# A delta-rule recurrence run over all eight heads at once, chunk by chunk, with its inputs prepared earlier and kept in DRAM

## The chip, the cores and the metric

The kernel runs on one core of one Trainium2 chip. The metric is the device time of one execution in microseconds.

## The reference, cut to what matters

Two layers, T = 1024 positions, D = 1024, all float32. Each layer makes three gated branches from one projection of the normed input and adds a projected mixture to the residual:

```python
h = rmsnorm(x, norm_g); proj = h @ w_in           # 1024 x 10256, split into the parts below
a = layernorm(dwconv31(a_val * sigmoid(a_glu)));  y_a = silu(a) * silu(a_z)      # 512 channels
q, k, v = silu(dwconv4(qkv));  q, k = l2norm(q) / sqrt(128), l2norm(k)           # 8 heads of 128
beta = sigmoid(b_beta);  g = -exp(a_log) * softplus(b_alpha + dt_bias)
o = gated_delta_rule(q, k, v, beta, g)            # per head: a chunked scan, each chunk a triangular
                                                  # solve, then S = d*S + k_dec^T v_new, o from S
y_b = rmsnorm(o, onorm_g) * silu(b_z)             # 1024 channels
y_c = gelu(c_u) * (tril(c_ws) @ layernorm(gelu(c_v)) + c_bs) * silu(c_z)         # 512 channels
gates = sigmoid(gate_logits)                      # 3 x 1024 channels
merged = gates[0]*(y_a @ a_proj) + gates[1]*(y_b @ b_proj) + gates[2]*(y_c @ c_proj)
x = x + merged @ w_out                            # after both layers: a final rmsnorm
```

## The kernel before, in words

Activations lie with channels on the 128 partitions and positions in the free dimension. A large product is made in float32r as three passes (high x high, high x low, low x high parts of both operands), so a step of a product is three matmuls of 128x512. A weight tile comes from DRAM into one of three `wr` buffers, ScalarE copies its high part and GpSimd subtracts the low part (`split`), into one of five `W` buffers. `U` hands out 24 units of 4 KB per partition, in rotation; `hrings` holds eight 8 KB buffers for the split input `hT` and what follows it. PSUM has four `pg` banks (large products), two `pa` and two `pr`.

A layer runs in stages:

1. Two plain column tiles (`half_first`), the sums of blocks of h, then **the pairs** (`pairs`): two column tiles of `w_in` at a time, by a seven-product block scheme (`STEPS`, 7 x 12 = 84 matmuls for what plainly takes 96), 28 steps per pair. VectorE adds the products together (L364, L367) and carries the convolutions' taps, doled out per step (`TAPS_FAST`, `todo.tap`). GpSimd makes the weights' sums and low parts. Thirty-one pairs: values, gates, z, conv inputs, k, q, v and, at the end, `N_LATE` = 3 more pairs of gates. What is finished goes to DRAM (`k_d`, `q_d`, `v_d`, `z_d`, `g_d`, `ya_d`, `yc_d`), as does a part of hT that the block sums overwrite (`store_b12`, `reload_b12`).
2. **The recurrence, head after head.** For each head: `head_decay` (decay matrix `gam`, on GpSimd and ScalarE's exponential), `head_keys` (transposes of k, copies, squares), `head_pairs` (products qk and kk of all 8 chunks of 128 positions, VectorE from PSUM; then blocks of 32 go to DRAM and come back in another order, `s1_d`), `head_sub` (30 small VectorE operations, then a second trip through `s2_d`), `head_fetch`, `head_inv` (six rounds of small TensorE products that make the inverse `zt`), `head_values` (transposes of q and v), `head_rec` (for each chunk the products `ks`, `pq`, `pz`, `ps`, `po`, each 128x128, one after another through VectorE and ScalarE) and `head_out` (norm, transposes, times z, to `yb_d`). `interleave` puts these steps between the filler: 16 plain gate tiles (`plain`, `product` with 48 matmuls each), then projection c. `PERIOD` = 32 filler steps lie between the starts of two heads, and the stage takes `PERIOD * H + RAMP + EXTRA` = 275 of them. The head that follows is prepared beside the one that runs.
3. The rest of projections c and a, then b (`proj_c`, `proj_a`, `proj_b`), each product times its gate tile from DRAM, added up in `mp`.
4. The output product (`out_steps`), the residual and the next layer's norm.

TensorE executes in the order written throughout. VectorE does so in the pairs, VectorE and ScalarE in the recurrence; the other queues are ordered by the framework's scheduler, which is told of priorities. All DMAs are issued from the SyncE queue (SP) in order, and a DMA waits there for the data it stores and for the buffer it fills.

## Time and profile before

| | |
|---|---|
| time, median of 3 runs (lowest, highest) | 2714.35 us (2713.1, 2715.22) |
| the profiled execution: time, span | 2714.88 us, 2713.2 us |
| busy: TensorE, VectorE, GpSimd, ScalarE | 95%, 61%, 53%, 46% of the span |
| DMA queue of SP | 316.92 MB, 38.3% of 16 engines' span |
| TensorE's mean granted clock | 0.985 |

The profile is of one execution. Matmuls are pipelined and their ends are modelled, so a busy TensorE is not one at its peak. Layer 0 ends its pairs at about 746 us and its recurrence at about 1120 us; layer 1 at about 2080 and 2457 us.

### The profile page before, as it was taken

How to read it: one execution, taken by the hardware profiler on the slowest of the kernel's cores; microseconds unless marked ns; L12 is line 12 of the kernel's file. 1: busy time of each engine (PE TensorE's matmuls, PEld its weight loads, DVE VectorE, ACT ScalarE, POOL GpSimd, SP SyncE). 2: the span in 40 equal slices, each digit the busy share in tenths (PEclk: the TensorE clock that was granted, in tenths of full speed). 3: DMA queues.
4: the chain of work that ended last, by engine and by line, in shares of the span. 5: the costliest groups of instructions: out<-in, count | busy, mean ns of one | idle time of the engine just before them, and what ended most of it. 6: DMA issues, size and time to landing. Idle time of an engine off the chain costs nothing.

```text
span 2713.2 us, 42607 instructions
## 1 busy us (share of the span) xinstructions
PE 2581.5 (95%) x15963; PEld 2127.4 (78%) x15963; DVE 1653.5 (61%) x2934; ACT 1256.8 (46%) x2996; POOL 1426.3 (53%) x1144
## 2 busy tenths in 40 slices
PE   7899999999899999999999989999998999999998
PEld 6687778878788787788867878787786878878887
DVE  6688988666545453445366888986564545444442
ACT  4433435565466665322134334365654666652221
POOL 7766667758533332363166767677674333224520
PEclk9999999999999999999999989999999999999999
DMA  4122233434633534553312223243435344445432
GB/s 155 47 63 86 86 93 123 133 102 124 189 104 109 140 106 150 173 177 130 126 65 55 66 75 94 86 155 109 125 122 180 106 124 123 114 152 187 155 124 78
DMA packets 361634, 319.64 MB, mean 118 GB/s; under 512 B 98930, under 2 KB 313556, under 8 KB 360404
## 3 DMA queue, kind: packets, MB, share of 16 engines
q1 hardware_dynamic: 361428, 316.92, 38.3%
q8 instruction: 126, 2.06, 0.3%
q14 instruction: 80, 0.66, 0.1%
HBM read 221.12 MB, written 95.75 MB: 117 GB/s over the span
## 4 chain that ended last, share of the span: by engine, by line
PE 77%; DVE 9%; POOL 4%; ACT 4%; DMA 3%; issue 3%; SPq 0%; DVEq 0%; POOLq 0%; ACTq 0%
PE ps L346 35%; PE ps L246 23%; PE ps L1261 6%; PE pa L753 2%; DVE pr L686 1%; DMA wr<-in_w_in_dram 1%; PE pr L986 1%; PE pr L1003 1%; PE pr L995 1%; DVE yc L1137 1%; POOL S L174 1%; PE ps L270 1%; PE pr L1012 1%; PE pa L802 1%; DVE nm L1075 1%
## 5 line engine op out<-in xcount | busy, mean ns | idle before, releaser
L174 POOL TENSOR_TENSOR S<-st,S 128x512 fp32r<-128x512 f32 x248 | 330.0, 1331 | 201.2 <-ACT S L173 200.8
L174 POOL TENSOR_TENSOR wl<-wr,wh 128x512 fp32r<-128x512 f32 (+2 forms) x164 | 201.5, 1245 | 357.9 <-ACT wh L173 216.4
L346 PE MATMUL ps<-hT,A 128*128 128x512 f32 x1488 | 366.3, 394 | 0.0
L686 DVE SCALAR_TENSOR_TENSOR pr<-o,dwT,pr 128x512 f32<-128x512 f32 (+7 forms) x480 | 357.1, 745 | 13.6 <-ACT pr L1057 3.4
L364 DVE TENSOR_TENSOR o<-o,ps 128x512 f32<-128x512 f32 x430 | 287.2, 682 | 117.5 <-PE ps L346 106.3
L246 PE MATMUL ps<-hT,wh 128*128 128x512 f32 x960 | 332.4, 427 | 0.0
L346 PEld LDWEIGHTS ps<-hT,A 128*128 128x128 f32 x1488 | 281.1, 190 | 59.1 <-issue 0.8
L173 ACT ACTIVATE S<-st 128x512 fp32r<-128x512 f32 x248 | 156.6, 631 | 362.8 <-PE ps L346 210.0
L174 POOL TENSOR_TENSOR A<-wr,A 128x512 fp32r<-128x512 f32 x186 | 248.1, 1334 | 26.7 <-ACT A L173 25.9
L686 DVE SCALAR_TENSOR_TENSOR pr<-o,cvT,pr 128x512 f32<-128x512 f32 (+3 forms) x288 | 211.8, 752 | 44.9 <-ACT pr L706 40.6
L346 PE MATMUL ps<-T,A 128*128 128x512 f32 x744 | 192.4, 408 | 16.8 <-DVE o L364 16.8
L246 PE MATMUL ps<-hT,wl 128*128 128x512 f32 x480 | 189.8, 396 | 0.4 <-POOL wl L174 0.3
L346 PE MATMUL ps<-hT,S 128*128 128x512 f32 x744 | 184.7, 394 | 0.0
L346 PEld LDWEIGHTS ps<-T,A 128*128 128x128 f32 x744 | 144.9, 197 | 50.1 <-issue 19.7
L173 ACT ACTIVATE A<-wr 128x512 fp32r<-128x512 f32 x186 | 117.0, 629 | 126.9 <-PE ps L346 118.0
L346 PE MATMUL ps<-T2h,S 128*128 128x512 f32 x496 | 168.3, 397 | 3.0 <-ACT T2h L173 3.0
L346 PE MATMUL ps<-T3h,S 128*128 128x512 f32 x496 | 166.7, 394 | 3.0 <-ACT o L360 3.0
L346 PE MATMUL ps<-T1h,S 128*128 128x512 f32 x496 | 165.8, 393 | 0.0
L346 PEld LDWEIGHTS ps<-hT,S 128*128 128x128 f32 x744 | 139.2, 190 | 29.0 <-issue 0.7
L246 PEld LDWEIGHTS ps<-hT,wh 128*128 128x128 f32 x960 | 152.5, 191 | 11.9
L173 ACT ACTIVATE wh<-wr 128x512 fp32r<-128x512 f32 (+2 forms) x164 | 85.6, 549 | 162.5 <-issue 113.2
L1261 PE MATMUL ps<-woh,mg 128*128 128x512 f32 x512 | 140.7, 391 | 0.0
(298 smaller groups left out, 5734.8 us busy)
## 6 DMA issues: line engine op xcount, KB each, us to landing
wr<-in_w_in_dram SPq DMA_DIRECT2D x160, 512.0 KB
g_d<-gth SPq DMA_DIRECT2D x32, 512.0 KB
g_d<-o SPq DMA_DIRECT2D x16, 512.0 KB
z_d<-o SPq DMA_DIRECT2D x16, 512.0 KB
v_d<-o SPq DMA_DIRECT2D x16, 512.0 KB
k_d<-o SPq DMA_DIRECT2D x16, 512.0 KB
q_d<-o SPq DMA_DIRECT2D x16, 512.0 KB
gam<-gc_d SPq DMA_DIRECT2D x16, 512.0 KB
```

Of the source, the lines that this page charges most:

```text
L173: act.activation(out=hi, in_=src, func=AF.Copy)
L174: lo_eng.tensor_tensor(out=lo, in0=src, in1=hi.bitcast(F32), op=ALU.subtract)
L246: pe.matmul(ps[h], lhsT=w[wi][:, k, :], rhs=rhs(h, ri, k), start=(k == 0 and i == 0), stop=(k == kt - 1 and i == 2))
L270: pe.matmul(ps[h][:, sl], lhsT=w[wi][:, k, :], rhs=rhs(h, ri, k)[:, sl], start=(k == 0 and i == 0), stop=(k == kt - 1 and i == 2))
L346: pe.matmul(ps, lhsT=wt[:, wi, k, :], rhs=blk(nb, ri, k), start=(k == 0 and i == 0), stop=(k == 3 and i == 2))
L364: dve.tensor_tensor(out=out, in0=other, in1=ps, op=ALU.add)
L686: dve.scalar_tensor_tensor(out=acc[:, lo:], in0=x[:, h * HALF + lo - s:(h + 1) * HALF - s], scalar=taps[s - 1], in1=acc[:, lo:], op0=ALU.m ...
L753: pe.transpose(tp[:, j * P:(j + 1) * P], src[:, half * 4 + j, :], ident)
L802: pe.matmul(tp[:, j], lhsT=kT[:, n], rhs=qT[:, n], start=True, stop=True)
L986: pe.matmul(ks, lhsT=kT[:, n], rhs=st, start=True, stop=True)
L995: pe.matmul(pz, lhsT=zt[:, n, :], rhs=rt, start=True, stop=True)
L1261: pe.matmul(ps[h], lhsT=mg[hh, ri, k // 4][:, k % 4, off:off + P], rhs=wo[k][wi][:, h * HALF:(h + 1) * HALF], start=(k == 0 and i == 0), s ...
```

## The change

The recurrence is no longer run head by head. Its inputs are made head by head during the pairs (`head_prep`, `head_values`, `head_sub`, `head_fetch`, `head_inv`, strung together in `whole_head`; a head starts every 56 steps from pair 18.5 on) and stored in DRAM by chunk: `kE_d`, `vn_d`, `qk_d`, `zt_d` beside `k_d`, `q_d`, `z_d`, all laid out chunk, partition, head, position, so that a head is written in rows of 512 bytes and a chunk of all heads read in rows of 4 KB. The keys' factor E is multiplied in by VectorE as it empties PSUM, in place of ScalarE's copy and GpSimd's product. The inversion's PSUM tiles move from `pr` to `pa`, since `pr` belongs to the convolutions there.

All 24 gate tiles are made as pairs, so there are 39 pairs, the last eight of them gates; `plain` and `use_gate_tile` go, and with them `store_b12` and `reload_b12`. After the pairs comes projection c alone, with `yc` and `mp` in hT's buffers; then `recurrence` over 8 chunks, each with `ks`, `pq`, `pz`, `ps`, `po` for four heads at a time, into one bank, and with projection a and the first half of projection b (positions 0 to 511) as filler at `REC_FILL` = 1.5 steps per slot. The half of b can begin when four chunks are stored. The output of a chunk (`output`, `store`) is split into SBUF directly, without `yb_d`. Then the second half of b, for which its weights are loaded and split again.

```diff
-PERIOD = 32
-RAMP = 17
+PREP_FIRST, PREP_EVERY = 18.5, 56
+REC_FILL = 1.5
+LAG_DECAY = 4
...
+    k_d, q_d, z_d, kE_d, vn_d, qk_d, zt_d = (dr.tile([NT, P, H, P], F32, name=f"{nm}_d")
+                                             for nm in ("k", "q", "z", "kE", "vn", "qk", "zt"))
...
+    def head_prep(s, r):
...
+        k_u, q_u = fetch_head(k_d, hd, "kT"), fetch_head(q_d, hd, "qT")
+        kT, qT = by_chunk(k_u), by_chunk(q_u)
+        sp.dma_start(out=gam, in_=gc_d[:, hd, :].partition_broadcast(P))
+        yield from wait(10)
...
+            tp = tok(kT, half).rearrange("p (n i) -> p n i", n=4)
+            for j in range(4):
+                n = half * 4 + j
+                act.activation(out=junk, in_=tp[:, j], func=AF.Square, accum_out=ssk[:, n:n + 1])
+            yield
+            dve.tensor_tensor(out=kE[:, hs], in0=tp, in1=bc(E[:, 1, hs, hd], 2, P), op=ALU.mult)
+            yield
+        save_head(kE_u, kE_d, hd)
...
-        p0 = pr.tile([P, HALF], F32, name="pr").rearrange("p (n i) -> p n i", n=8)
+        p0 = pa.tile([P, HALF], F32, name="pa").rearrange("p (n i) -> p n i", n=8)
...
+    def recurrence(l, r, yb, fed):
...
+        load(0, "vn", "zt", "kE", "qk", "k", "q")
+        yield
...
+            if n + 1 < NT:
+                load(n + 1, "k", "q", "vn", "zt", "kE")
...
+            def ks(g):
+                if n:
+                    p = bank(pr, "pr")
+                    for j in range(4):
+                        hd = g.start + j
+                        pe.matmul(p[:, j], lhsT=kT[:, hd], rhs=st[:, hd], start=True, stop=True)
+                    for j in range(4):
+                        hd = g.start + j
+                        dve.scalar_tensor_tensor(out=vn[:, hd], in0=p[:, j], scalar=E[:, 3, n, hd:hd + 1],
+                                                 in1=vn[:, hd], op0=ALU.mult, op1=ALU.add)
...
+            A, B = SLOTS
+            for i, (f, g) in enumerate(((ks, A), (ks, B), (pq, A), (pz, A), (pq, B), (pz, B), (ps, A), (po, A),
+                                        (ps, B), (po, B))):
+                f(g)
+                if i == 8:
+                    squares(A)
+                beside()
+                if i == 5:
+                    F(c.pop("vn"), c.pop("zt"))
+                    load_z(n)
+                    if n + 1 < NT:
+                        load(n + 1, "qk")
                 yield
...
+        def whole_head(s):
+            yield from head_prep(s, r)
+            values = head_values(s)
+            for _ in range(14):
+                next(values, None)
+                yield
+            for _ in head_sub(s):
+                next(values, None)
+                yield
+            run(values)
+            yield from wait(8)
+            yield from head_fetch(s)
+            yield from wait(8)
+            for _ in head_inv(s):
+                yield from wait(3)
+        prep = [(late(lambda s=s: whole_head(s)), int(PREP_FIRST * 28 + PREP_EVERY * s.hd), 1) for s in hs]
...
+        add_glu(3), add_z(4), add_z(6), add_gates(1), add_kq(0), add_kq(1)
         at["a_norm"] = len(specs)
...
+        add_v(0), add_az(0), add_az(2), add_kq(2), add_v(2), add_kq(3), add_gates(1)
+        add_kq(4), add_v(4), add_kq(5), add_gates(1), add_kq(6), add_v(6), add_kq(7)
+        add_gates(8)
...
+        feed = projections()
+        run(steps(feed, 8 * NT))
+        with tc.manual_schedule(engines={getattr(mybir.EngineType, e) for e in B_ENG}):
+            credit, fed = 0.0, 8 * NT
+            for _ in recurrence(l, r, yb, lambda: fed):
+                credit = min(credit + REC_FILL, 2.0)
+                while credit >= 1 and (fed < 16 * NT or len(r.stored) >= 4):
+                    credit -= 1
+                    fed += 1
+                    next(feed, None)
+        run(feed)
```

## Rows read from the trace of the kernel before

**Rows 1.** The page's first part: engine, busy us (share of the span) xinstructions.
```profile
PE 2581.5 (95%) x15963; PEld 2127.4 (78%) x15963; DVE 1653.5 (61%) x2934; ACT 1256.8 (46%) x2996; POOL 1426.3 (53%) x1144
```

**Rows 2.** The chain of waits in order of time: start us, us, what.
```profile
356.80 175.99 PE ps L346 x768
...
737.03 8.30 DMA inv<-s
...
1902.42 4.25 DMA wr<-in_w_in_dram
```

**Rows 3.** Windows, recurrence and pair stages' ends: stretch, length, busy (instructions), clock, DMA share, GB/s.
```profile
746.00:1120.00 374.00, 356.74 (x3747) 295.36 (x3748) 172.15 (x538) 228.44 (x785) 117.58 (x112) 0.99 0.44 124
...
2080.00:2457.00 377.00, 355.93 (x3747) 295.08 (x3748) 174.16 (x541) 229.36 (x787) 120.63 (x115) 1.00 0.44 127
...
704.00:750.00 46.00, 36.27 (x235) 29.59 (x233) 24.67 (x56) 21.26 (x60) 19.57 (x17) 0.93 0.71 217
2045.00:2095.00 50.00, 40.92 (x349) 33.16 (x348) 24.18 (x56) 26.72 (x75) 22.46 (x22) 0.97 0.64 209
```

**Rows 4.** The timeline of TensorE in the recurrence: start us, us, engine, line, operation.
```profile
863.98 0.60 PE L753 MATMUL pa<-ident,kT 128*128 128x128 f32 x4
864.34 0.71 PE L246 MATMUL ps<-hT,wh 128*128 128x512 f32 x2
...
866.92 0.39 PE L991 MATMUL pr<-st,qT 128*128 128x128 f32 x2
867.14 1.06 PE L802 MATMUL pa<-qT,kT 128*128 128x128 f32 x8
867.96 0.70 PE L246 MATMUL ps<-hT,wh 128*128 128x512 f32 x2
```

**Rows 5.** Groups of TensorE, 746 to 1120 us: busy, mean ns | idle before, releaser.
```profile
L958 PE MATMUL pr<-inv,gam 64*64 64x64 f32 x128 | 9.1, 221 | 0.0
...
L914 PE MATMUL pr<-inv 32*32 32x32 f32 x512 | 6.3, 199 | 11.7 <-DVE inv L910 11.7
...
L936 PE MATMUL pr<-inv,gam 32*32 32x32 f32 x256 | 5.6, 192 | 4.4 <-DVE sub L853 3.7 <-DVE inv L931 0.7
```

**Rows 6.** Groups of VectorE, 760 to 1120 us: six heads' pairs, seven heads' head_sub.
```profile
L855 DVE TENSOR_TENSOR sub<-sub 128x16 f32<-128x16 f32 (+14 forms) x105 | 34.8, 331 | 1.9
L856 DVE TENSOR_REDUCE sub<-sub 128x8 f32<-128x16 f32 (+14 forms) x105 | 24.1, 230 | 3.6
...
L824 DVE SCALAR_TENSOR_TENSOR gam<-pa,Wn,gam 128x128 f32<-128x128 f32 x48 | 13.4, 342 | 0.0
...
L803 DVE TENSOR_TENSOR qk<-pa,gam 128x512 f32<-128x512 f32 x12 | 8.3, 690 | 1.3 <-ACT junk L771 1.0 <-PE pa L802 0.3
```

**Rows 7.** Windows in the pair stage of layer 0, columns as in rows 3.
```profile
460.00:540.00 80.00, 80.00 (x355) 66.24 (x354) 54.80 (x81) 42.64 (x71) 57.73 (x46) 1.00 0.46 145
...
560.00:600.00 40.00, 35.95 (x177) 29.50 (x176) 25.71 (x42) 30.51 (x70) 24.38 (x22) 1.00 0.34 110
...
240.00:260.00 20.00, 14.72 (x59) 11.59 (x57) 18.40 (x26) 4.44 (x7) 8.83 (x8) 0.83 0.23 78
...
400.00:420.00 20.00, 20.00 (x90) 16.55 (x89) 19.50 (x30) 5.72 (x10) 14.76 (x12) 1.00 0.20 53
```

**Rows 8.** Groups of ScalarE, 760 to 1120 us.
```profile
L997 ACT ACTIVATE vh<-pr,W 128x128 f32<-128x128 f32 x64 | 23.5, 367 | 15.2 <-PE pr L995 13.1
...
L785 ACT ACTIVATE gam<-gam,ng 128x128 f32<-128x128 f32 x48 | 17.3, 392 | 0.1
...
L771 ACT ACTIVATE junk<-kE 128x128 f32<-128x128 f32 x48 | 14.8, 309 | 1.1
```

**Rows 9.** The timeline of ScalarE at a change from exponential to Silu.
```profile
610.94 1.28 ACT L717 ACT_TABLE_LOAD   x1
612.24 1.06 ACT L717 ACTIVATE o<-o 128x1024 f32<-128x1024 f32 x1
```

More of the change, by code (lines that the diff above doesn't have):

```diff
@@ L551, in drop_sum @@
                 free.rotate(len(us))
-    def reload_b12():
-        for i in range(2):
-            hT[1, i, 0] = hrings[1, i, 0].tile([P, 4, HALF], F32R, name="hT")
-            with tc.issue_after(last_load[0].ins):
-                sp.dma_start(out=hT[1, i, 0].rearrange("p k t -> p (k t)").bitcast(F32), in_=b12_d[i])
-        yield
     class Record:
@@ new lines, in head_prep @@
+        nk2 = sm.tile([P, 8], F32, name="nk2", bufs=1)
+        dve.tensor_scalar(out=nk2, in0=ssk, scalar1=EPS, scalar2=None, op0=ALU.add)
+        Wt = r.W[:, hd, :]
+        dve.reciprocal(out=Wt, in_=nk2)
+        dve.tensor_tensor(out=Wt, in0=Wt, in1=beta[:, :, hd], op=ALU.mult)
+        Wn = sm.tile([P, 8], F32, name="Wn", bufs=1)
+        dve.tensor_scalar(out=Wn, in0=Wt, scalar1=-1.0, scalar2=None, op0=ALU.mult)
+        s.nk = sm.tile([P, 8], F32, name="nk")
+        pool.tensor_tensor(out=s.nk, in0=nk2, in1=phalf, op=ALU.pow)
@@ L797, in head_pairs @@
+        yield from wait(LAG_DECAY)
+        qk_u = U("qk")
+        qk = by_chunk(qk_u)
         mT = gam
@@ L917, in head_inv @@
         yield
[L918 removed]
+        q0 = pa.tile([P, HALF], F32, name="pa").rearrange("p (n i) -> p n i", n=8)
         for n in range(NT):
@@ L1215, in proj_c @@
             th = fetch(g_d[2, m], "gcl")
-            if m in (0, 2):
-                pair = hrings[0, m // 2, 1].tile([P, 2, T], F32, name="mp")
-                mp.extend((pair[:, 0], pair[:, 1]))
-            elif m >= 4:
-                mp.append(th)
-            yield from product(w(), y_rhs(yc), 4, gate_mul(th, mp[m]), w.ahead)
-            if m < 4:
-                F(th)
-        for hi, lo in yc:
-            F(hi, lo)
+            yield from product(w(), y_rhs(yc), 4, gate_mul(th, lambda h: mp_tile(mp, h, m)), w.ahead)
+            F(th)
     def proj_a(ya, mp, w):
@@ L1229, in proj_a @@
             th = fetch(g_d[0, m], "gal")
-            yield from product(w(), y_rhs(ya), 4, gate_mul(th, th), w.ahead, done_with(ya) if m == NT - 1 else None)
-            pool.tensor_tensor(out=mp[m], in0=mp[m], in1=th, op=ALU.add)
+            yield from product(w(), y_rhs(ya), 4, gate_mul(th, lambda h: th[:, hsl[h]]), w.ahead)
+            for h in range(2):
+                out = mp_tile(mp, h, m)
+                pool.tensor_tensor(out=out, in0=out, in1=th[:, hsl[h]], op=ALU.add)
             F(th)
-    def done_with(ys):
-        return lambda k: F(*ys[k])
@@ L1425, in layer @@
-                    (steps(second_head, S_SECOND[0]), *at_step("head", S_NEXT[4], 0.5))])
-        tc_dve.__exit__(None, None, None)
-        def plain():
-            br, m = order[n_gates]
-            for i, pss in enumerate(half_first((w(),), h_rhs, 8)):
-                if i in (4, 6):
-                    w.ahead()
-                yield
-            use_gate_tile(br, m)(pss[0])()
-            for br, m in order[n_gates + 1:]:
-                yield from product(w(), h_rhs, 8, use_gate_tile(br, m), w.ahead)
-            yield from proj_c(yc, mp, w)
-            yield from proj_a(ya, mp, w)
@@ L1487, in used, with projections, more_wo @@
             wo.append((hi, lo))
-        run(proj_b(yb, mp, mg, w, used))
+        def projections():
+            yc, ya = [], []
+            load_split(yc_d, yc)
+            for h in range(2):
+                for q in range(2):
+                    mp[h, q] = hrings[h, 1, q].tile([P, 4, HALF], F32, name="mp")
+            yield from proj_c(yc, mp, w)
+            load_split(ya_d, ya)
+            yield from proj_a(ya, mp, w)
+            yield from proj_b(yb, mp, mg, w, 0, pool)
+            for p in range(4):
+                F(yb[0, 0, p], yb[0, 1, p])
+        feed = projections()
[9 more added lines that the diff above has]
+        run(feed)
+        def used(k):
+            if k % 2:
+                F(yb[1, 0, k // 2], yb[1, 1, k // 2])
+                if len(wo) < 8:
+                    load_wo()
+        def more_wo():
+            for _ in range(6):
+                load_wo()
+                yield
+        interleave(proj_b(yb, mp, mg, w, 1, dve, used), [(more_wo(), 4, 8)])
         g_bc = load_gain(norm_g[l + 1] if l + 1 < DEPTH else final_g)
```

536 lines of the change are left out of this document (252 added, 284 removed).

## Prediction

> **What bounds the kernel now.** The page's first part comes first: TensorE is busy 95% of the span and no other engine over 61% [rows 1]. A busy TensorE need not stream, so the chain of waits is read next: where nothing holds it, 768 matmuls of 128x512 take 175.99 us, 0.229 us each with some records missing; the 175.99 us of pieces and the windows (90 started or ended in 20 us) both fit 0.227 us, which I use; a step of three is 0.68 us [rows 2, 7]. By that price a stage is split into work and standing still.
>
> The recurrence of layer 0 takes 374.0 us (layer 1: 377.0) [rows 3]. It holds 275 filler steps by the code (PERIOD x 8 + RAMP + EXTRA), 825 matmuls or 187 us. The heads' own TensorE work: a lone f32 128x128 matmul occupies 0.22 us, four in a row 0.82, four transposes 0.36 [rows 4]. Eight heads need 38 recurrence matmuls each (304 x 0.22 = 67), 24 groups of four for qk and kk (20), 228 transposes (21) and eight inversions. The inversion's six products cost at most four times L914's 6.3/8 and twice L958's 9.1/8, 5.4 us a head, 43 in all [rows 5]. Sum 151; I take 148, since the first head's qk and some edges fall outside. So 374 - 187 - 148 = 39 us stand still, 42 in layer 1. The groups name 16 of them: inversions waiting for VectorE (11.7 and 4.4 us) [rows 5]. The other 23 us, 6% of the stage, are seams between short f32 work and filler. Just ahead, at the end of the pairs, 46.0 - 36.27 = 10 us and 50.0 - 40.92 = 9 us are idle; the chain there holds 8.30 us of one inv load [rows 2, 3]. These 39 + 10 + 42 + 9 = 100 us are all that a reordering here can win; later stages stream.
>
> **The change, part by part.** *Gate tiles as pairs.* Sixteen gate tiles per layer leave `product` (16 x 48 = 768 matmuls) and become eight pairs (8 x 84 = 672): 96 fewer, 192 for both layers, at 0.227 us: **-43.6 us**. This is the one certain term, since both forms stream at the same price. The matmuls of projection b stay 384: halves change their order and load and split its weights twice, eight more loads of 512 KB with two ScalarE and two GpSimd operations each. That hides behind 24 matmuls (5.4 us) per tile; uncovered it would be a load of 4.25 us each [rows 2], 34 per layer. The removed b12 store and reload, yb round trip and plain start lie in the stalls already taken out.
>
> *The old stalls go: -100 us.* What is late instead is costed in three places.
>
> *(a) Head preparation in the pair stage.* Its TensorE work is moved, not added: 24 transposes 2.2, qk and kk 3.3, inversion 5.4, about 10.5 us a head after rounding down. A head starts every 56 steps, so two pairs (38.1 us) and one head share 48.6 us. A head asks VectorE for L855 34.8/7, L856 24.1/7, L824 13.4/6, L803 8.3/6 and again 1.4 for the decayed keys, now made there: 5.0 + 3.4 + 2.2 + 1.4 + 1.4 = 13.4 us plus small ones [rows 6]. Two pairs with q, k, v convolutions ask 68% of 38.1, or 26 us (54.80 of 80) [rows 7]. Together 39.5 of 48.6, 81%. ScalarE: 8 exponentials 2.9, 16 squares 4.9, 8 copies 2.9, some 13 small copies priced like the squares 4.0, 14.7 at least; two pairs ask 53% of 38.1, 20.3 [rows 7, 8]. Together 72%. GpSimd gives the product of the keys away and gains nothing else of size; it stands at 72% (57.73 of 80). The head's DMAs come along: four loads and four stores of 512 KB and the small ones of the two block passes, 4 MB or 84 GB/s beside today's 145 at 46% share [rows 7], 230 at about 73%. All go through SP in order, so a store that waits for its engine holds up the weights behind it, which have three load buffers and five split pieces of lead. No engine is over its time on average. But VectorE and TensorE keep the order written, the pieces of two heads alternate on the two banks of `pa`, and the fifteen steps of `head_sub` put 8.4 us of VectorE work into 10 us that also carry taps. So the cost is waiting. Bounds: no reason allows less than the 16 us per layer that today's inversions wait for VectorE; at worst six heads' 291 us lose the 26% of the window at 240 us, where VectorE was busy 18.40 of 20: 77 us [rows 7]. Nearest is the window at 560 us, where layer norm works through transposes, ScalarE and `pa` as the heads will: 4.05 of 40 us idle, 10% [rows 7]. On the nine convolution pairs among the heads (9 x 24.3 us) that is 22; two heads in gate pairs add their inversion waits, 4. I take **26 per layer**.
>
> *(b) Two hand-overs.* yc can be loaded only into hT's buffers, the last of which frees with the last pair; ya only into yc's. A load of 512 KB costs 4.25 us where it was the wait, the reload through SP's queue 8.30 for 128 KB [rows 2]; a split behind it needs one VectorE operation of 1024 columns (twice L803's 0.69) and one ScalarE operation of about 1.1, 2.5 us [rows 6]. A four-tile product covers 18 matmuls, 4.1 us, before the last tile is needed: 4.25 + 2.5 - 4.1 is 3 us each, 6 for both, to 16 if both meet a queue like inv's. I take **8 per layer** (4 to 16).
>
> *(c) The recurrence.* A chunk has 40 f32 matmuls in fours (8.2), 8 transposes (0.7) and 15 filler steps (10.2): 19.1 us, eight of them 153. Between `ks` and `pz`, `pz` and `ps`, `ps` and the next `ks` lie three slots of 1.8 us; a link needs 0.82 plus four operations of 0.34 to 0.37 [rows 4, 6, 8], 2.3 us: covered. Seams at 6% cost 9. The eight tiles per chunk that share `pa` collide about twice for 0.5 us, 8. Filler ends when proj_a does, in chunk 4, since proj_b may not start before four chunks are stored: eight slots bare, where sixteen copies (5.9) and the chain outlast 7.3 us of matmuls by about 4. Start and tail 3. **24 per layer**; low 15 without the collisions, high 52: a chunk loads seven tiles of 512 KB and 1.4 MB for the filler, 4.9 MB; at the 217 GB/s of the stretch where loads were the wait, 22.6 us, 28 more [rows 3].
>
> Sum: 2713.2 - 43.6 - 100 + 2 x (26 + 8 + 24) = 2685.6 us span; the execution lay 1.7 over its span, and 0.5 over the median: **2687 us**.
>
> [...] Exponentials and the convolutions' Silu need different tables: in the trace a load of 1.28 us stands before each change, and 612.24 - 610.94 shows nothing behind it but the load [rows 9]. Today only the first heads' exponentials meet Silu; then those of seven heads do, in two blocks each. [...]
>
> **Rivals.**
> - *Preparation chokes the pairs (the other side).* VectorE at 92% held TensorE up for 26% of the window at 240 us; at 400 us it was busy 19.50 of 20 with even work, and TensorE never stopped [rows 7]. It decides from 40 us per layer (5.0 a head); at 77 the time is 2687 + 102 = **2789**.
> - *Loads set the recurrence's pace:* 4.9 MB per 19.1 us is 257 GB/s, against 217 at 71% share today [rows 3]; large rows speak for less. 52 in place of 24: **2743**.
> - *Table changes land on TensorE's path,* because the squares and copies queued behind them hold `pa`. Two per head and layer cost 7 x 2 x 2 x 1.28 = 36, four 72: 2723 to **2759**. For: two banks; against: ScalarE has 28% left.
> - *Waits stay at their low ends:* 16, 4 and 15: 2687 - 46 = **2641**. For: the first heads' preparation in today's gate pairs.
> - *The change does not relieve anything:* the new waits eat the 43.6 us, **2709 to 2720**.
>
> **How the numbers follow.** Forecast 0.46 (2650 to 2708); low waits 0.13; nothing gained 0.08; preparation 0.16; loads 0.09; tables 0.08. A difference under 0.2% (5.4 us) is about what this kernel's measurement cannot tell from none. Faster 0.59, same 0.08, slower 0.33. Low waits end around 2630; above 2760 lies the greater part of the preparation case, 0.10. Range 2630 to 2760; the forecast's own is 2650 to 2708.
>
> **What would show it.** 3,276 matmuls at the pairs' line per layer and none of plain gate tiles; a pair stage longer by about 152 us of pairs and 67 of preparation; a recurrence near 180 us per layer beside today's 374. Wrong would be: TensorE waiting in the pairs for VectorE's `o` or ScalarE's `junk` by over 40 us per layer; `recurrence` matmuls waiting for DMA; more than 60 table loads in the stage. If the matmul count does not fall, the certain term is gone.

## The result: slower, and the profile after

The changed kernel takes **2904.03 us** (median of 4 runs, 2901.36 to 2909.61) beside 2713.72 us of the kernel before: the ratio is **1.0705, 95% interval 1.0686 to 1.0723**. The forecast was 2687 us with a range of 2630 to 2760; it missed by 217 us and has the wrong sign.

The page's first part for the changed kernel, to be read beside [rows 1]: TensorE fell from 95% to 90% of a longer span, VectorE kept its 61%.

```profile
PE 2606.8 (90%) x15771; PEld 2140.1 (74%) x15771; DVE 1772.8 (61%) x3002; ACT 1318.5 (45%) x3100; POOL 1599.6 (55%) x1320
```

Windows of the changed kernel, columns as in [rows 3]: both pair stages, what lies between the last pair and the output product in both layers, and both recurrences.

```profile
64.40:1086.30 1021.90, 912.00 (x5830) 742.25 (x5829) 686.34 (x1170) 502.82 (x1120) 621.70 (x510) 0.95 0.43 121
1499.20:2516.50 1017.30, 909.12 (x5829) 739.35 (x5828) 683.49 (x1164) 501.18 (x1118) 615.36 (x509) 0.95 0.43 122
...
1086.00:1370.00 284.00, 261.76 (x1428) 222.18 (x1427) 138.75 (x259) 119.04 (x369) 133.54 (x110) 0.96 0.57 191
2517.00:2805.00 288.00, 261.85 (x1422) 221.81 (x1422) 136.09 (x259) 120.02 (x371) 135.06 (x111) 0.95 0.56 189
1153.00:1323.00 170.00, 160.33 (x1012) 140.92 (x1011) 84.11 (x206) 84.28 (x312) 88.13 (x75) 0.98 0.52 179
2584.00:2753.00 169.00, 159.31 (x1007) 140.03 (x1006) 84.13 (x206) 84.29 (x312) 87.71 (x75) 0.98 0.52 179
```

The recurrence takes 170 and 169 us where [rows 3] have 374 and 377. From the last pair to the output product 284 and 288 us were measured. The forecast's sum has 287 to 288 there (535.9 us in layer 0 before, less 174.3 of plain tiles, 67 of preparation and 39 of standing still, and 32 of new waits), so nothing of the miss lies behind the pairs. The pair stage was to take 681.5 - 10 + 152.5 + 67 + 26 = 917 us in layer 0. By the same cut (from the first pair to the first inversion, which before begins at 745.94 us in layer 0 and at 2085.13 in layer 1) it was to take 674 - 9 + 152.5 + 67 + 26 = 910.5 us in layer 1. It takes 1021.9 and 1017.3: **105 and 107 us too much**, nearly the whole of the 217. In it TensorE is not busy for 109.9 and 108.2 us, and its granted clock is 0.95; the trace has two levels, 1.00 (from 632 to 638 us) and 0.50 (from 625 to 630 us).

What TensorE waited for in the changed kernel, both layers together (engine, tile and line, releaser: us in total, times, longest):

```profile
PE pa L726 <- DVE kE L761: 65.6, 14, 9.5
PE pa L894 <- DVE inv L890: 43.7, 14, 4.0
PE ps L230 <- ACT y L157: 21.8, 4, 8.4
PE pa L944 <- ACT inv L940: 18.5, 12, 1.9
PE ps L330 <- DVE o L348: 16.9, 7, 5.2
```

L726 are the transposes of `tok`, L761 scales the keys and is the new VectorE operation, L894 and L944 are products of the inversion. The pairs' own line L330 hardly waits for VectorE's sums: 16.9 us, as before. The groups of VectorE, 440 to 1086 us:

```profile
L838 DVE TENSOR_TENSOR sub<-sub 128x16 f32<-128x16 f32 (+14 forms) x120 | 72.6, 605 | 3.3
L839 DVE TENSOR_REDUCE sub<-sub 128x8 f32<-128x16 f32 (+14 forms) x120 | 27.6, 230 | 4.1
...
L761 DVE TENSOR_TENSOR kE<-pa,E 128x512 f32<-128x512 f32 x16 | 10.4, 683 | 7.0 <-ACT junk L759 7.0
```

The substitution's multiply (L838) takes 605 ns where [rows 6] have 331 for the same shapes; its reduce still takes 230. One such place, first in VectorE's timeline:

```profile
615.07 1.09 DVE L838 TENSOR_TENSOR sub<-sub 128x72 f32<-128x72 f32 x1
616.19 0.23 DVE L839 TENSOR_REDUCE sub<-sub 128x8 f32<-128x72 f32 x1
616.46 0.95 DVE L838 TENSOR_TENSOR sub<-sub 128x80 f32<-128x80 f32 x1
...
618.79 0.30 DVE L838 TENSOR_TENSOR sub<-sub 128x88 f32<-128x88 f32 x1
...
619.41 0.32 DVE L838 TENSOR_TENSOR sub<-sub 128x96 f32<-128x96 f32 x1
...
623.73 0.29 DVE L839 TENSOR_REDUCE sub<-sub 128x8 f32<-128x128 f32 x1
623.94 1.28 DVE L761 TENSOR_TENSOR kE<-pa,E 128x512 f32<-128x512 f32 x2
```

GpSimd's timeline at the same time:

```profile
614.77 1.29 POOL L271 TENSOR_TENSOR st<-wr,st 128x512 f32<-128x512 f32 x1
616.03 1.29 POOL L158 TENSOR_TENSOR A<-wr,A 128x512 fp32r<-128x512 f32 x1
...
618.50 0.96 POOL L882 MEMSET zt<- 128x1024 f32 x1
```

And TensorE's:

```profile
619.29 1.53 PE L330 MATMUL ps<-hT,A 128*128 128x512 f32 x6
624.67 1.12 PE L726 MATMUL pa<-ident,qT 128*128 128x128 f32 x4 [3.85 <-DVE kE L761]
...
628.15 0.63 PE L330 MATMUL ps<-T2h,S 128*128 128x512 f32 x1
628.58 0.63 PE L330 MATMUL ps<-T2l,S 128*128 128x512 f32 x1
...
637.44 0.39 PE L330 MATMUL ps<-T1l,S 128*128 128x512 f32 x1
637.66 0.39 PE L330 MATMUL ps<-T1h,S 128*128 128x512 f32 x1
```

with the windows of the two stretches behind the wait:

```profile
624.60:631.00 6.40, 6.33 (x18) 5.19 (x19) 4.83 (x8) 3.58 (x12) 2.85 (x3) 0.54 0.50 114
632.00:638.00 6.00, 6.00 (x27) 4.67 (x25) 4.30 (x8) 4.55 (x14) 4.21 (x4) 1.00 0.62 174
```

Three things are to be seen. First, the 128x72 and 128x80 multiplies end within 0.1 us of GpSimd's operations on weights (616.16 beside 616.06, 617.41 beside 617.32), while the larger 128x88 and 128x96 take 0.30 and 0.32: GpSimd writes a memset as they begin, and that does not hold them up. Over the whole execution 135 of the 240 multiplies began while GpSimd was at a weight's sum or low part; they take 0.86 us on average. The other 105 take 0.30, the 17 that began beside the memset 0.31. Second, behind the last round stand the next head's keys at 623.94. Until they are out of PSUM, TensorE stands before the next transposes (3.85 us at 624.67), although it has pair matmuls behind them in its queue. Third, when it goes on, its matmuls begin 0.43 us apart at a granted clock of 0.54, and from 632 us 0.22 to 0.23 apart at 1.00: the lower clock comes on top of the wait.

### The profile page after: what moved, and what is told of

Same layout as the page of the kernel before. It is cut to its first block, busy times and chain, and to the rows that moved or that the text cites. A ratio compares the mean times of both kernels' runs of the same rounds, so it can differ in the third digit from the quotient of the medians.

```text
span 2899.6 us, 42862 instructions
## 1 busy us (share of the span) xinstructions
PE 2606.8 (90%) x15771; PEld 2140.1 (74%) x15771; DVE 1772.8 (61%) x3002; ACT 1318.5 (45%) x3100; POOL 1599.6 (55%) x1320
## 5 line engine op out<-in xcount | busy, mean ns | idle before, releaser
L158 POOL TENSOR_TENSOR S<-st,S 128x512 fp32r<-128x512 f32 x312 | 414.2, 1328 | 263.2 <-ACT S L157 261.7
L348 DVE TENSOR_TENSOR o<-o,ps 128x512 f32<-128x512 f32 x542 | 362.2, 681 | 320.7 <-PE ps L330 306.8
L330 PE MATMUL ps<-hT,A 128*128 128x512 f32 x1872 | 488.1, 407 | 0.0
L330 PEld LDWEIGHTS ps<-hT,A 128*128 128x128 f32 x1872 | 358.9, 196 | 76.1 <-issue 0.6
L158 POOL TENSOR_TENSOR wl<-wr,wh 128x256 fp32r<-128x256 f32 (+2 forms) x132 | 154.3, 1183 | 239.2 <-ACT wh L157 128.8
L330 PE MATMUL ps<-T,A 128*128 128x512 f32 x936 | 241.7, 404 | 17.6 <-DVE o L348 16.9
L330 PE MATMUL ps<-hT,S 128*128 128x512 f32 x936 | 241.0, 397 | 0.0
L330 PE MATMUL ps<-T2h,S 128*128 128x512 f32 x624 | 225.5, 411 | 3.1 <-ACT T2h L157 3.0
L330 PE MATMUL ps<-T3h,S 128*128 128x512 f32 x624 | 226.8, 415 | 1.5 <-POOL S L158 1.2
L330 PEld LDWEIGHTS ps<-T,A 128*128 128x128 f32 x936 | 178.0, 195 | 56.8 <-issue 19.9
L330 PE MATMUL ps<-T1h,S 128*128 128x512 f32 x624 | 207.6, 392 | 0.0
L230 PE MATMUL ps<-y,wh 128*128 128x512 f32 x512 | 174.8, 421 | 26.0 <-ACT y L157 21.8
L330 PEld LDWEIGHTS ps<-hT,S 128*128 128x128 f32 x936 | 171.5, 188 | 35.1 <-issue 1.0
L282 POOL TENSOR_TENSOR st<-wr 128x512 f32<-128x512 f32 x78 | 103.1, 1322 | 151.1 <-DMA wr<-in_w_in_dram 145.8
L1298 PE MATMUL ps<-yb,wh 128*128 128x512 f32 x512 | 168.1, 410 | 7.3 <-ACT wh L157 7.3
L838 DVE TENSOR_TENSOR sub<-sub 128x16 f32<-128x16 f32 (+14 forms) x240 | 147.4, 614 | 6.5
L330 PEld LDWEIGHTS ps<-T2h,S 128*128 128x128 f32 x624 | 123.6, 198 | 30.3 <-ACT T2h L157 3.4
```

What stands on the lines that cost most here:

```text
L158: lo_eng.tensor_tensor(out=lo, in0=src, in1=hi.bitcast(F32), op=ALU.subtract)
L230: pe.matmul(ps[h], lhsT=w[wi][:, k, :], rhs=rhs(h, ri, k), start=(k == 0 and i == 0), stop=(k == kt - 1 and i == 2))
L282: pool.tensor_tensor(out=s1, in0=a21, in1=a22, op=ALU.add)
L330: pe.matmul(ps, lhsT=wt[:, wi, k, :], rhs=blk(nb, ri, k), start=(k == 0 and i == 0), stop=(k == 3 and i == 2))
L348: dve.tensor_tensor(out=out, in0=other, in1=ps, op=ALU.add)
L838: dve.tensor_tensor(out=pd[:, :, 0:i + 1], in0=bc(mb3[:, 0:i + 1, i], 1, 8), in1=tt[:, :, 0:i + 1], op=ALU.mult)
```

## The experiments

Times are of one run each where no interval is given; with them ran the kernel before, at 2710 to 2718 us. Four runs of one kernel lie 7 to 15 us apart (changed kernel, e17, e18, e19), so differences under 15 us are not read from single runs. All start from the changed kernel.

**Keys 14 steps later.**

```diff
-        yield from wait(10)
+        yield from wait(24)
         pool.affine_select(out=gam, ...
```

> Each head's first transposes and its keys come 14 steps later, so that they fall behind the previous head's substitution on VectorE instead of beside it; everything else of the head moves with them. Theory (step (a) was mis-sized, because VectorE is late with the keys while it is in the substitution and so holds both small PSUM banks): the wait of the transposes for VectorE's keys falls from 67 us in all to under 20, and the time by 40 to 90 us, to 2815 to 2865 us. Rival (the preparation's own matmuls and its transfers are the loss, wherever they lie): no change beyond 10 us, 2894 to 2914. Rival (a head's later steps are the loss, and moving the head only moves the wait): under 20 us of gain, with the wait now at another line of the head.

2939.49 us: **35 us slower**, outside all three ranges. Its waits of GpSimd, then TensorE:

```profile
POOL gam L749 <- DMA gam<-gc_d: 110.8, 14, 9.9
...
PE pa L726 <- DVE kE L761: 91.7, 14, 10.9
...
PE pa L938 <- issue: 53.7, 6, 10.2
```

The wait for the keys grew, and a new one came before the inversion's 64x64 products. So the collision with one neighbour's substitution was not the whole of it; the theory in this form fell. What GpSimd does at L749 is taken up below.

**Most of the substitution left out.**

```diff
         for i in range(1, 16):
-            dve.tensor_tensor(out=pd[...], ...)
-            dve.tensor_reduce(out=tt[...], ...)
+            if i == 1:
+                dve.tensor_tensor(out=pd[...], ...)
+                dve.tensor_reduce(out=tt[...], ...)
```

> Leaves out 14 of the 15 rounds of the substitution on VectorE (multiply and reduce), with all its transfers and steps kept. Theory (VectorE late in the substitution holds the banks): some 200 us of VectorE's work go, the wait for the keys falls under 15 us, the time by 60 to 130 us, to 2775 to 2845. Rival (the inversion's round trips over DRAM and the table loads are the loss): under 25 us of gain, over 2880. Rival (hand-overs behind the pairs): no change, 2894 to 2914.

2843.72 us, 60 less: the low end of the theory. The wait for the keys fell as told (6.8 us in all), but 176 us of VectorE's busy time bought only 60, and the inversion's wait for VectorE grew from 43.7 to 62.1.

**Keys by ScalarE.**

```diff
-            dve.tensor_tensor(out=kE[:, hs], in0=tp, in1=bc(E[:, 1, hs, hd], 2, P), op=ALU.mult)
+            for j in range(4):
+                n = half * 4 + j
+                act.activation(out=kE[:, n], in_=tp[:, j], func=AF.Copy, scale=E[:, 1, n, hd:hd + 1])
```

> The scaled keys are taken out of PSUM by ScalarE, in eight operations of 128x128 with the scale of each chunk, instead of by VectorE's two of 128x512; VectorE keeps the substitution. The result is the same. Theory: the transposes no longer wait for VectorE, that wait of 67 us goes to under 10 and ScalarE takes no more than 25 us of it, so 2815 to 2870. Rival (ScalarE is late too, with the norms' squares, the exponentials and their table loads): the wait is there under ScalarE's name, at least 45 us of it, and the time is 2885 to 2930.

2862.94 us, 41 less, inside the theory's range; but 36.1 of the 65.6 us came back under ScalarE's name, more than it allowed.

**Only the transfers of the preparation.**

```diff
-            yield from head_prep(s, r)
-            ... values, substitution, inversion ...
+            k_u, q_u = fetch_head(k_d, hd, "kT"), fetch_head(q_d, hd, "qT")
+            ... stores of k_u, q_u and v in the places of kE, qk, zt and vn ...
```

> Leaves out all that the engines do to prepare a head between the pairs, and keeps its large transfers to and from DRAM (keys, queries and values in; four arrays out); the pairs, the recurrence and the hand-overs are whole. By the forecast's own sizes this takes away 67 us of matmuls and 26 us of stalls a layer, 186 in all: 2718. Theory (the forecast's whole miss of 217 us lies in the engines' work of the preparation): 134 us of matmuls, 52 us of forecast stalls and most of the 217: 2500 to 2560. Rival (traffic of 512-byte rows, the pairs themselves, or the hand-overs hold the miss): 2690 to 2730. Between 2560 and 2690 both have a share.

2530.58 us, **373 less**. That expectation took 67 us for the matmuls, which is only the part that moved; the eight heads' whole is the forecast's 8 x 10.5 = 84, so its rival should have read 2904 - 2 x (84 + 26) = 2684, and both ranges for the theory 34 us lower. The answer is the same: windows of its two pair stages,

```profile
63.00:899.50 836.50, 786.77 (x3463) 643.00 (x3461) 531.61 (x769) 348.34 (x592) 575.98 (x446) 0.98 0.45 138
1316.00:2144.80 828.80, 785.26 (x3463) 643.05 (x3461) 525.25 (x762) 345.39 (x590) 568.53 (x445) 0.98 0.46 139
```

against 1021.9 and 1017.3 us with the heads. What the run leaves out, the engines' work of the preparation with its loads of the gates and its small block transfers, costs 185 and 189 us a layer where 84 + 26 = 110 were forecast. Of it 60 and 65 us are time in which TensorE is not busy (109.9 and 108.2 less 49.7 and 43.5). Another 31 and 34 are the clock: the trace has the lower level, 0.50, for 102 and 99 us with the heads and for 41 and 31 without, and half of the difference is lost. The rest, 94 and 90, is its matmuls at full speed beside the 84. The large transfers, rows of 512 bytes, are at most a small part of the loss: what is left of the miss without the heads is 30 and 28 us (worked out below). That part has waits of its own, which the changed kernel hardly has (1.2 us at L330):

```profile
PE ps L330 <- POOL A L158: 20.7, 10, 3.8
PE ps L330 <- POOL S L158: 14.4, 6, 3.5
```

All of them lie between 582 and 784 us and between 1831 and 2029 us, while the heads' transfers run (the last stores are issued at 779 and 2024 us), and GpSimd there waits for weights from DRAM (243.5 us in all, 145.8 in the changed kernel).

**No table loads.**

```diff
-                act.activation(out=gam[:, n], in_=gam[:, n], func=AF.Exp, scale=-1.0, bias=r.ng[...])
+                act.activation(out=gam[:, n], in_=gam[:, n], func=AF.Tanh, scale=0.0)
```

> Leaves out the decay matrix: in place of the exponential ScalarE takes the hyperbolic tangent of zero times the same tile, as many operations of the same size, so that no table has to be loaded for them. The rest is whole. Theory (VectorE's lateness and its waits are the loss): about 24 of 43 table loads go and the time stays within 12 us of 2904, 2892 to 2912, since ScalarE's waits at TensorE are 20 to 25 us in all and most of them are the length of its operations. Rival (the table loads lie on TensorE's path): 24 times 1.28 us or more, 2840 to 2875.

2885.29 us, 19 less, between the two. 30 of 43 loads go, 38 us of ScalarE's time. But the 128 operations also became shorter, 0.30 us in place of 0.39, which is another 12: so the tables are worth 19 us at most, a small part of the loss.

**No inversion.**

```diff
-        ... six products and their evacuations ...
+        for _ in range(6):
+            yield
```

> Leaves out the six products of the inversion and their evacuations (the inverse is stored as zeros), and keeps the substitution and every transfer. Theory (the inversion's waits are a loss of their own: 77 us in the pair stages of both layers beside 86 us of matmuls, and the clock that falls behind each wait): 150 to 190 us less, 2715 to 2755. Rival (the inversion only shows where VectorE is late, and what does not wait there waits at the next line): 85 to 115 us less, 2790 to 2820.

2800.27 us, 104 less, the rival's range, and no more than TensorE's busy time lost (2606.8 to 2499.2 us; 86 by the forecast's price). The first line of its waits shows why:

```profile
PE pa L726 <- DVE kE L761: 117.2, 14, 11.0
```

The heads stall nearly as long as before (65.6 + 43.7 + 18.5 us), only at one place instead of three.

**One operand in the multiply.**

```diff
-            dve.tensor_tensor(out=pd[...], in0=bc(mb3[...], 1, 8), in1=tt[...], op=ALU.mult)
+            dve.tensor_scalar(out=pd[...], in0=tt[...], scalar1=0.0, scalar2=None, op0=ALU.mult)
```

> Leaves out the substitution's product: its multiply becomes a multiply of one operand by a constant, of the same shape and as often, with the sums behind it unchanged. Theory (a multiply with two operands in SBUF waits until GpSimd's operation ends, with one it does not): its mean falls from 614 ns to under 330, some 70 us of VectorE's busy time go, and the time falls by 25 to 60 us, 2844 to 2879. Rival (the multiply is slow by its shape or its strides): its mean stays above 500 ns and the time within 10 us of 2904.

2911.51 us, no gain, and a mean of 598 ns in the stretch from 440 us, as before the edit (605): two operands are not what matters. But neither is the shape: of its 240, the 151 that began beside any GpSimd operation take 0.86 us and the 89 others 0.20. The rival's reason fell too, though its numbers came. The pair on three banks below settles it.

**VectorE's load spread.** The keys as in e3, and:

```diff
+SUB_EVERY, TAPS_LATE, LATE_FROM = 2, 0.43, 520
-                    credit += TAPS_SLOW if step // 28 in slow else TAPS_FAST
+                    credit += TAPS_LATE if step > LATE_FROM else TAPS_SLOW if step // 28 in slow else TAPS_FAST
             for _ in head_sub(s):
-                next(values, None)
-                yield
+                for _ in range(SUB_EVERY):
+                    next(values, None)
+                    yield
```

> The keys scaled by ScalarE as in the run of that name (2863 us), and VectorE's load spread: a round of the substitution every second step instead of every step, and from step 520 on the convolutions' taps at 0.43 per step instead of 0.65. The result is the same. Theory (VectorE is asked for more than a step holds for some fifteen steps of each head, and its order is fixed, so that the next head's inversion and products come late): the inversion's wait for VectorE falls from 45 us to under 20 and the time to 2800 to 2845. Rival (these waits are round trips over DRAM and between engines, as long whatever VectorE's load): 2850 to 2880.

2876.96 us, the rival's range, and no gain over the run that it starts from (2863). The inversion's wait for VectorE did fall under 20 us, but again TensorE stood 53.7 us before the 64x64 products, as in e1.

**The gates earlier.** The load of `gam` becomes the first of a head's transfers and the mask moves behind the keys; in e9 on top of e8, in e10 on top of e3:

```diff
+        sp.dma_start(out=gam, in_=gc_d[:, hd, :].partition_broadcast(P))
         k_u, q_u = fetch_head(k_d, hd, "kT"), fetch_head(q_d, hd, "qT")
-        sp.dma_start(out=gam, in_=gc_d[:, hd, :].partition_broadcast(P))
         yield from wait(10)
-        pool.affine_select(out=gam, ...)
         ...
         save_head(kE_u, kE_d, hd)
+        pool.affine_select(out=gam, ...)
```

> The run with VectorE's load spread (2877 us), and in it the load of each head's gates is the first of the head's transfers and GpSimd's mask on it comes six steps later. In that run, and in the one with later keys, TensorE stood 54 us before the inversion's 64x64 products for nothing that the trace names; in the latter GpSimd waited 111 us in all for that load, in front of the inversion's two small copies. Theory (GpSimd's queue, held by the mask, holds the inversion): the 54 us go, and with them what hangs behind: 2790 to 2840. Rival (the stall has another cause, as the small copies' own time behind the weight sums): it stays above 30 us, 2860 or more.

> The keys scaled by ScalarE (2863 us) and the earlier load and later mask of the gates, without the spread. Theory (GpSimd's wait for the gates also makes weight sums late and VectorE with them): 2835 to 2860. Rival (in this order nothing of the path stands behind the mask): 2858 to 2868.

2866.46 us (e8 had 2877) and 2855.17 (e3 had 2863), both differences too small to be read. e9 met its rival: the stall before the 64x64 products (L940) is still 44.8 us, and another stands before the products ahead of them:

```profile
PE pa L928 <- ACT inv L922: 35.2, 8, 9.0
PE pa L940 <- issue: 30.5, 4, 7.8
...
PE pa L940 <- POOL st L272: 14.3, 2, 7.4
```

e10 lies in its theory's range, which shows nothing at this size. e9's ScalarE timeline shows what the theory had left out:

```profile
592.65 1.28 ACT L775 ACT_TABLE_LOAD   x1
598.61 2.15 ACT L775 ACTIVATE gam<-gam,ng 128x128 f32<-128x128 f32 x7 [4.68 <-POOL gam L764]
600.67 1.10 ACT L872 ACTIVATE vn<-pa,nk 128x128 f32<-128x128 f32 x4
...
603.23 0.78 ACT L922 ACTIVATE inv<-pa 32x256 f32<-32x256 f32 x2
```

and TensorE's the price:

```profile
593.14 0.69 PE L918 MATMUL pa<-inv,gam 32*32 32x32 f32 x32
...
603.65 0.66 PE L928 MATMUL pa<-inv 32*32 32x32 f32 x3 [7.56 <-ACT inv L922]
```

The exponentials of the next head wait in ScalarE's queue for GpSimd's mask, and behind them stands the evacuation for which the inversion waits (an evacuation is the copy out of PSUM): a product ready at 593.83 is fetched at 603.23. The mask begins at 597.48, 10.4 us after its load was issued. For this mask the trace names no releaser; for 9 of the 16 it names the load, 73.3 us in all.

**The solution in PSUM, and its control.** Both on top of e10, e11 with the first line alone: the control with three banks for the pairs' products instead of four, and the fourth bank for the substitution's solution `tt`:

```diff
-    pg = ctx.enter_context(tc.tile_pool(name="pg", bufs=4, space=PSUM))
+    pg = ctx.enter_context(tc.tile_pool(name="pg", bufs=3, space=PSUM))
+    pt = ctx.enter_context(tc.tile_pool(name="pt", bufs=1, space=PSUM))
-        pool.tensor_copy(out=tt, in_=eye8)
+        s.tp = pt.tile([P, HALF], F32, name="pt")[...]
+        act.activation(out=s.tp, in_=eye8, func=AF.Copy)
...
-            dve.tensor_tensor(out=pd[...], in0=bc(mb3[...], 1, 8), in1=tt[...], op=ALU.mult)
-            dve.tensor_reduce(out=tt[...], ...)
+            dve.tensor_tensor(out=pd[...], in0=bc(mb3[...], 1, 8), in1=s.tp[...], op=ALU.mult)
+            dve.tensor_reduce(out=s.tp[...], ...)
...
+        act.activation(out=tt, in_=s.tp, func=AF.Copy)
```

> As the run before it, with three PSUM banks instead of four for the pairs' products; it is the control for the next one. Theory: a product takes 2.7 us and its sums 0.7 to 1.4 us on VectorE, so that three banks do while VectorE is on time: within 10 us of the run before. Rival (the fourth bank is what lets TensorE run on while VectorE is late): 30 us or more slower, with the wait at the pairs' line for VectorE's sums.

> As the control with three banks, with the substitution's solution kept in the free bank of PSUM, so that its multiply reads one operand from SBUF and one from PSUM; ScalarE copies it in and out. The result is the same. Theory (the multiply waits for GpSimd's operations because it takes both of its operands through SBUF): its mean falls from over 600 ns to under 400, VectorE gets 50 us or more back, and the time is 20 to 60 us under the control. Rival (it is slow by its shape, or the sums of weights slow it in another way): a mean above 550 ns and no gain.

2888.74 us, 34 over e10 (the rival: 38.5 us of waits for VectorE's sums where e10 has 15.6), and 2864.89, **24 under its control**. Groups of VectorE in the control,

```profile
L839 DVE TENSOR_TENSOR sub<-sub 128x16 f32<-128x16 f32 (+14 forms) x240 | 146.8, 612 | 6.5
```

and with the solution in PSUM:

```profile
L841 DVE TENSOR_TENSOR sub<-sub,pt 128x16 f32<-128x16 f32 (+14 forms) x240 | 66.6, 277 | 5.4
L842 DVE TENSOR_REDUCE pt<-sub 128x8 f32<-128x16 f32 (+14 forms) x240 | 56.8, 236 | 8.2
```

The same multiply with one operand in PSUM takes 277 ns, although 158 of the 240 began beside GpSimd's work on weights; 80 us of VectorE's time come back and bring 24.

**No taps beside the heads.** The three taps of the convolutions of q, k and v are left out:

```diff
+            if len(taps) > 3:
                 dve.scalar_tensor_tensor(out=acc[:, lo:], in0=x[...], scalar=taps[s - 1], ...)
```

> The changed kernel without the three taps of the convolutions of keys, queries and values, which are 144 VectorE operations of 0.75 us a layer; their first and last steps on ScalarE stay. Theory (the preparation stalls because VectorE is asked for convolutions and substitution at once): the waits of the heads for VectorE, 124 us in both layers, mostly go, and the time falls by 80 to 150 us, 2754 to 2824. Rival (the head's own chain between TensorE, ScalarE, VectorE and two PSUM banks is too long for the steps it has, whatever else VectorE does): under 40 us, 2864 or more.

2866.19 us, 38 less for about 216 us of VectorE's work: the rival's range. The wait for the keys is still 57.9 us; that of the inversion for ScalarE doubled to 37.9.

**Heads beside pairs without taps.** On e10, and with the solution in a bank of the convolutions in e15:

```diff
-PREP_FIRST, PREP_EVERY = 18.5, 56
+PREP_FIRST, PREP_EVERY = 21.5, 52
-        add_v(0), ..., add_kq(3), add_gates(1)
-        add_kq(4), add_v(4), add_kq(5), add_gates(1), add_kq(6), add_v(6), add_kq(7)
-        add_gates(8)
+        add_v(0), ..., add_kq(3)
+        add_kq(4), add_v(4), add_kq(5), add_kq(6), add_v(6), add_kq(7)
+        add_gates(10)
```

> The keys scaled by ScalarE and the earlier gates (2855 us), with two pairs of gate tiles moved from between the convolutions' pairs to the end, and the heads begun at pair 21.5 instead of 18.5 and every 52 steps instead of 56: the convolutions are over by pair 25, when three of eight heads have begun. The result is the same. Theory (convolutions and substitution together are too much for VectorE): 2795 to 2830. Rival (the chain of a head is too long whatever lies beside it, and heads now follow closer): 2845 to 2880.

> The run with late heads, and the substitution's solution in one of the two PSUM banks of the convolutions, which stand idle then; ScalarE copies it in and out. The result is the same. By the pair of runs on three banks this is worth 24 us. Theory: the multiply's mean falls under 330 ns and the time by 15 to 35 us against the run with late heads. Rival (beside gate pairs VectorE has time to spare, so a faster multiply is worth nothing): within 8 us.

2913.84 us, **59 more** than e10, beyond its rival's range too, and 2886.55, 27 less than e14, with the multiply at 276 ns: its theory. Relieving VectorE by this order of the pairs does not pay: in e14 GpSimd waits 127.5 us for the gates, and TensorE 43.2 us before L927 for an evacuation of ScalarE. The order, the later start and the 52 steps were changed at once, and no run separates them.

**The gates 12 steps ahead.** In e17 on top of e9; in e18 with e3's keys and the solution in PSUM, the heads where the change has them; in e19 on top of e15:

```diff
-PREP_FIRST, PREP_EVERY = 18.5, 56
+PREP_FIRST, PREP_EVERY = 506.0 / 28, 56        # 12 steps earlier; in e19 590.0 / 28, 52
...
         sp.dma_start(out=gam, in_=gc_d[:, hd, :].partition_broadcast(P))
+        yield from wait(12)
         k_u, q_u = fetch_head(k_d, hd, "kT"), fetch_head(q_d, hd, "qT")
```

> The run with spread load and the earlier gates (2866 us), with the load of each head's gates 12 steps ahead of its other transfers. In the traces that load of 512 KB lands 8 to 10 us after SP issues it, and GpSimd stands 4 to 10 us in front of the mask each time, 73 us and more in that run, with the previous head's small copies and the memset of its inverse behind it in the queue. Theory (GpSimd's queue is the path: what waits there holds the inversion): GpSimd's wait for the load goes under 20 us, TensorE's 46 us before the 64x64 products and part of the 37 us before the products ahead of them go, 2800 to 2835. Rival (the waits only move again): 2850 to 2875.

> The heads where the changed kernel has them, with the keys scaled by ScalarE, the gates' load 12 steps ahead, and the substitution's solution in one of the convolutions' two PSUM banks; no spread. The result is the same. Theory (the three causes add: 41, about 8 and 24 us): 2815 to 2845. Rival (the convolutions need both of their banks beside the heads): 2850 to 2890.

> The run with late heads and the solution in PSUM (2887 us), with the gates' load 12 steps ahead. There GpSimd waited 122 us for that load and TensorE 63 us before products that need GpSimd's copies or what follows them. Theory (late heads lost only by what stood behind GpSimd's wait): 2790 to 2830, the best of the three. Rival (heads 52 steps apart are too close whatever GpSimd does): 2850 or more.

**e17: 2814.8 us**, 89 under the changed kernel and 52 under e9; to before 1.037 (1.0355 to 1.0386). e18: 2859.43 (1.0538, 1.0516 to 1.056); e19: 2883.87 (1.0621, 1.0603 to 1.0638), both their rivals. e17's timeline of ScalarE:

```profile
583.34 2.44 ACT L776 ACTIVATE gam<-gam,ng 128x128 f32<-128x128 f32 x8 [2.09 <-POOL gam L765]
...
595.45 0.77 ACT L923 ACTIVATE inv<-pa 32x256 f32<-32x256 f32 x2
```

and its waits:

```profile
POOL gam L765 <- DMA gam<-gc_d: 90.9, 16, 7.1
...
PE pa L904 <- ACT inv L899: 48.6, 10, 6.1
```

The time is the theory's, the way only half: GpSimd still waits 90.9 us for the load, not under 20. What changed is what stands behind: the exponentials now run 12 us ahead of the evacuation L923 instead of 5 in front of it, and TensorE's waits at L928 and L940, 80 us in e9, are 2 (L929 and L941 here). A part came back at L904, which waits 48.6 us for ScalarE; at 586 us the trace shows that evacuation right behind the same exponentials. In e18 the bank taken from the convolutions is a likely reason that the faster multiply brings nothing (VectorE's taps wait 142 us for ScalarE's start of a convolution, 44 in e10); no run shows it apart.

## Why the prediction was wrong

- **The certain term held.** 3,276 matmuls at the pairs' line per layer and none of plain gate tiles: 192 fewer, by the forecast's price -43.6 us.
- **The old stalls went, and the recurrence was right:** 170 and 169 us where near 180 was forecast. It holds 10 us of idle time, not 24. *Loads set the recurrence's pace* did not happen: 179 GB/s at 52% share, and in neither recurrence does a wait of TensorE name a DMA (3.6 us of its waits stand behind a copy of weights that had waited 5.2 us for their load).
- **(b) and (c) together** came out, partly by luck. TensorE is idle for 22 and 26 us a layer where 8 + 24 were forecast: 10 in the recurrence, but 13 in the 67 us of projection c alone, behind ScalarE's splits (21.8 us before L230 in both layers), where (b) had 8. The clock, which the forecast left out, takes another 12 and 14: 24 and 27 us at the lower level. And the sum leaves 148 - 67 = 81 us of the heads' own matmuls in the recurrence, though (c) itself needs only 8 x 8.9 = 71.
- **The 100 us hold 5 twice:** the wait of 5.28 us before layer 1's first inversion lies both in the 377 us from 2080 and in the 50 us to 2095.
- **(a) is the step that failed**, in its sentence "Nearest is the window at 560 us ... I take **26 per layer**". It saw that the cost would be waiting and mis-sized it. What e4 leaves out costs 185 and 189 us a layer where 84 + 26 were forecast; against 26 us of waiting stand 91 and 99, of them 60 and 65 idle and 31 and 34 of lower clock. Even the upper bound of 77, the rival *Preparation chokes the pairs*, was short. The rival had the place and the sign and got 0.16.
- **Why the window at 560 us misled** is argued from the rows and not shown by a run of its own. Layer norm has one chain through the two banks of `pa`; here two heads take turns on them, and each use is closed by an engine that has a queue of its own work in a fixed order. TensorE's queue is fixed too, so that each late evacuation stops the pairs (3.85 us at 624.67). The sum of the loads (81% and 72%) said that no engine was over its time, and that was true: 57% of VectorE, 55% of ScalarE from 440 to 1086 us. It was not the question.
- **The causes that were shown, with their prices:** keys on VectorE behind the substitution 41 us (e3); the multiply beside GpSimd 24 to 27 (e12 against e11, e15 against e14); tables 19 at most (e5); the gates' load through GpSimd's mask and ScalarE's exponentials 52 in the order of e9 (e17). They do not add: e18 has three of them out and is no faster than e10. Convolutions beside the heads are worth 38 (e13), and the forecast's case of VectorE at 92% is only that much of it.
- **What stays open.** Without the heads the pair stage is still 30 and 28 us longer than the forecast's sizes make it (681.5 - 10 - 17 + 152.5 and 674 - 9 - 17 + 152.5; 17 is the part of the heads that the stage held before). 19 and 16 of them are the waits for GpSimd shown in e4. They lie beside the transfers and none in the last five pairs, which speaks for the transfers of that run and against the eight added pairs; no run leaves the transfers out. Since the changed kernel hardly has these waits, 185 and 189 are rather too small. And e17 still pays 284 us over e4 for the heads: 184 are matmuls by the price measured above, some 100 stalls. That two banks are too few for two heads is not shown: the order that was to show it (e16, the inversions in the convolutions' banks as well) has engines wait for each other for ever, and so no time.
- **The test named for it looked at the wrong line:** waits for `o` or `junk` over 40 us a layer. `o` came to 16.9 us in all; the waits stood at the heads' own tiles.
- **Table loads.** 43 loads of 1.28 us, with 0.02 us of idle time before a load and 0.01 behind it (medians): the rows show nothing but the load. The 30 that e5 leaves out are 38 us of ScalarE's time.

## What to carry to other kernels

Work whose chain goes through several engines is not priced by their load but by each hand-over: which engine empties the PSUM bank, what stands ahead of that in its queue, and what this waits for. In e9 a load that no matmul waits for held a matmul through two other engines' queues (TensorE stood 7.56 us before the one at 603.65). When leaving out a step moves the wait to the next line, as in e2 and e6, look in the queues for the instruction that waits, and move what stands behind it. And before a chain is moved under a stage that streams, run that stage with the chain's transfers alone: one run (2530.58 us) gave a size that no row of the kernel before could.

## What the runs showed of the hardware

VectorE's multiply of two tiles in SBUF took 0.86 us on average when it began beside a GpSimd operation on weights (1.2 to 1.35 us each) and 0.31 beside a GpSimd memset; with GpSimd idle it took 0.28 (changed kernel). A multiply by a constant, SBUF to SBUF, took 0.86 beside GpSimd and 0.20 alone, and here the memset did slow it, to 0.63 on average in seven cases (e7). With one operand in PSUM the multiply of two tiles took 0.28 and 0.26 (e12). The reduce of one SBUF tile took 0.23 throughout. Why it took longer beside GpSimd no run shows. The forecast had priced the multiply from [rows 6], 0.33 us, where 5 of the 105 began beside an operation on weights; in the changed kernel 135 of 240 do, and a head's fifteen take 9.1 us in place of 5.0.

Waits cost twice here: after the one of 3.85 us TensorE's matmuls began 0.43 us apart at a granted clock of 0.54, later 0.22 to 0.23 apart at 1.00. Over a pair stage the granted clock of 0.95 in place of 0.98 added 31 to 34 us to 60 to 65 of idle time; the forecast had priced the idle time alone.
